# A state-space mixer in chunks of 256 tokens, recomputed in chunks of 128 with the state carried at each token tile

## The chip, the cores and the metric

The kernel runs on one core of one Trainium2 chip, as one launch. The metric is the device time of a whole execution in microseconds. A core has five engines that run their own instruction streams side by side: TensorE (PE: matmuls; its weight loads are listed as PEld), VectorE (DVE), ScalarE (ACT), GpSimd (POOL) and SyncE (SP, which only issues DMAs here). They wait for each other through semaphores. Matmuls write to PSUM, which has eight banks of 512 fp32 numbers in each of 128 partitions; everything else lives in SBUF.

## The reference, cut to what matters

The program is one transformer-like layer on 1024 tokens of width 1024: an input projection that feeds a sparse attention and a state-space mixer, a gated merge of both, and a feed-forward part. The change touches the state-space mixer alone. It has 32 heads of 64 channels in 8 groups of 4 heads; a group shares B and C with 128 states.

```
dt = softplus(dt_raw + dt_bias);  A = -exp(a_log);  X = xh * dt;  dA = dt * A
a_cum = cumsum(dA) within a chunk                       # chunk: any length gives the same result
CB = C B^T;  L[l, s] = exp(a_cum[l] - a_cum[s]) for s <= l, else 0
y_diag = (CB * L) X                                     # within the chunk
states = B^T (exp(a_cum[last] - a_cum) * X)             # what the chunk adds to the state
h(next chunk) = h * exp(a_cum[last]) + states           # the carried state
y_off = exp(a_cum) * (C h)                              # what the earlier chunks give
y = (y_diag + y_off + d_skip * xh) * silu(z)            # then a norm over all channels
```

The reference uses chunks of 64 tokens. The result doesn't depend on the length of a chunk, so a kernel may choose it: a longer chunk means larger triangles in y_diag, a shorter one more state updates.

## The kernel before

**Layout.** All activations are stored transposed, channels in the partitions and tokens in the free dimension, in halves of 512 tokens. The state-space part works in chunks of QC = 256 tokens, that is, two token tiles of 128 (P), so NCH = 4 chunks.

**Prologue (dt_part, L490).** It forms dt, dA, the running sum acum within each chunk of 256 (a triangular matmul, L507, plus a matmul with ones that adds the first tile's total to the second tile, L508), the chunk totals (L510 and L511), decay = exp(total - acum) and cdec = exp(total), one per chunk. It stores acum and exp(acum), transposed, to DRAM (d_ac and d_ea).

**The stage (L1086 to L1094).** The steps run over the 8 groups g, and in each group over the 4 chunks c: 32 steps. `weave` (L824) interleaves three generators by turns: `ssd_in` of this step, `ssd_out` of the step before, and `beside`, the filler, which is dense matmul work: the gate projection (L1059 to L1066, tile pw) and then the attention's output projection (L1074 to L1083, tile poa), 6 matmuls of 512 columns at a time (`dense_steps`, L231). Both have 128 turns of filler in all, four for a step.

**ssd_in (L949)** has four turns.
- It loads B^T, C^T and xs (tile ld), and the row acum broadcast over the partitions (al, L961). ACT computes exp(-relu(acum_s - acum_l)) from it in three pieces: for the source tokens of the first tile all 256 target tokens (in place in al, L967 and L969), for those of the second tile the 128 later ones (tile M, L966 and L969).
- PE multiplies B and C into the bank pcb: 256 columns for the first source tile (L972) and 128 for the second (L973). DVE applies a mask of 384 columns (triangle, ones, triangle; L975) to give cbm, and multiplies al and M by cbm (L977).
- PE transposes xs into px (L983); DVE multiplies by dt to give X (L985).
- Except in the last chunk, PE transposes B into pbn (L992), ACT copies it to bn (L994), and POOL forms Xd = X * decay (L996).

**ssd_out (L1000)** has four turns too.
- It loads z and, except in the first chunk, exp(acum), broadcast (d_ea, L1010), into yt (a part of tile zy). PE forms y_diag in the bank pyd: for each of two pairs of heads j, and each head e of a pair, which fills one half of the output rows, the first source tile gives 256 columns (L1016) and the second adds to the last 128 (L1017).
- Except in the last chunk, PE sums both tiles' state products in the bank pst (L1023, twice 256 columns).
- Except in the first chunk, PE forms C h in the bank pyo from the chunk's starting state st (L1028, twice 256 columns), and DVE computes yt = yt * pyo + pyd (L1030, L1031); the first chunk only copies pyd (L1033). DVE adds d_skip * xs (L1035), POOL multiplies by z (L1037), and the result is stored to d_y.
- ACT squares it and DVE sums the squares (L1041 to L1047). The state is updated: POOL multiplies st by cdec (L1051), DVE adds pst (L1053); the first chunk only copies pst (L1049).

**What sets the order.** The program's text gives the order in which instructions are offered; a planner (L55) then simulates all engines on a time line with its own cost estimates and chooses each engine's order from it. Only the parts under `in_order` keep the order of the text, and the state-space stage isn't one of them. On the chip each engine runs its list in that fixed order. PSUM banks are tiles of two pools: five banks (bank) for the state-space work, three (bank_d) for the dense matmuls. SBUF tiles come from arenas of equal slots (Q, R, EV, H), and a tile's first use waits until the slot's former tile has been read for the last time.

Of the kernel before, what the change touches and what calls it, by code (L numbers as in the profile page):

```python
# [10 lines left out]
F32 = mybir.dt.float32  # L11
# [6 lines left out]
P = 128  # L18
# [50 lines left out]
def build(tc, a, dbg=None, stop=99, slots=None):  # L69
# [117 lines left out]
    mask384 = con.tile([P, 384], F32, name="mask384")  # L187
    tri = mask384[:, 0:128]
# [186 lines left out]
    def const_loads():  # L375
        SP.dma_start(mask384, a["mask384"])
# [113 lines left out]
    def dt_part():  # L490
# [7 lines left out]
        for m in (15, 13, 11, 9, 7, 5, 3):  # L498
# [6 lines left out]
        pcv = pc[:, 0:256].rearrange("p (c t h) -> p c t h", c=NCH, t=2)  # L505
        dAv = dA.rearrange("p (c t) h -> p c t h", t=2)
        T.matmul(pc[:, 0:256], tri, dA.rearrange("p t h -> p (t h)"), start=True, stop=False)  # L507
        T.matmul(pcv[:, :, 1, :], ones, dAv[:, :, 0, :], start=False, stop=True)  # L508
        ptot = bank("ptot")
        T.matmul(ptot[:, 0:128], ones, dAv[:, :, 0, :], start=True, stop=False)  # L510
        T.matmul(ptot[:, 0:128], ones, dAv[:, :, 1, :], start=False, stop=True)  # L511
        acum = con.tile([P, NT, 32], F32, name="acum")
        V.tensor_copy(acum.rearrange("p t h -> p (t h)"), pc[:, 0:256])
        tot = tmp[1][:, 1, 0:NCH, :]
        V.tensor_copy(tot.rearrange("p c h -> p (c h)"), ptot[:, 0:128])
        decay = con.tile([P, NT, 32], F32, name="decay")
        V.tensor_tensor(decay.rearrange("p (c t) h -> p c t h", t=2), tot[:, :, None, :].to_broadcast([P, NCH, 2, 32]),
                        acum.rearrange("p (c t) h -> p c t h", t=2), op=OP.subtract)
        S.activation(decay, decay, AF.Exp)
        cdec = con.tile([P, NCH, 32], F32, name="cdec")  # L520
# [428 lines left out]
    def ssd_in(c, g, out):  # L949
# [12 lines left out]
        late_ = Q("M")  # L962
        Mv = [al[:, 0:2], al[:, 2:4], late_.rearrange("p (h l) -> p h l", h=4)]
        for h in range(4):
            hd = 4 * g + h
            S.activation(Mv[2][:, h], al[:, h, 128:256], AF.Relu, scale=-1.0, bias=acum[:, 2 * c + 1, hd:hd + 1])  # L966
            S.activation(al[:, h], al[:, h], AF.Relu, scale=-1.0, bias=acum[:, 2 * c, hd:hd + 1])  # L967
        for m in (al, Mv[2]):
            S.activation(m, m, AF.Exp, scale=-1.0)  # L969
        yield  # L970
        pcb = bank("pcb")
        T.matmul(pcb[:, 0:256], BT[:, 0:128], CT, start=True, stop=True)  # L972
        T.matmul(pcb[:, 256:384], BT[:, 128:256], CT[:, 128:256], start=True, stop=True)  # L973
        cbm = Q("cbm", (P, 384))
        V.tensor_tensor(cbm, pcb[:, 0:384], mask384, op=OP.mult)  # L975
        for m, cb in ((al, cbm[:, 0:256]), (Mv[2], cbm[:, 256:384])):
            V.tensor_tensor(m, m, cb[:, None, :].to_broadcast(list(m.shape)), op=OP.mult)  # L977
# [513 lines left out]
```

## Time and profile before

| | |
|---|---|
| median of 3 runs | 2521.27 us (2516.20 to 2521.45) |
| profiled execution, its own time | 2517.42 us |
| its span, from the first to the last instruction | 2515.6 us |
| granted clock of TensorE, mean over the span | 0.978 |
| matmul records on PE, all of the program | 11946 |
| DVE, ACT, POOL instructions | 3056, 2300, 833 |
| HBM read and written | 252.68 MB and 86.27 MB, 135 GB/s over the span |

The profile is one execution of the program. Its page gives the busy time of each engine as a share of the span; the chain of work that ended last, followed back from the last instruction to what released each step; and groups of instructions by line of the kernel, written as out<-in by the program's tile names, with partitions x elements, the count, the busy time, the mean length in ns, and the idle time of the engine just before them. A matmul's record lasts until its result has left the array, so records of back-to-back matmuls overlap, and PE can be busy all the time without being at its peak. The trace answers closer questions: windows (busy time of each engine in a stretch), waits (who waited for whom), and a timeline.

### The profile page before, as it was taken

How to read it: one execution, taken by the hardware profiler on the slowest of the kernel's cores; microseconds unless marked ns; L12 is line 12 of the kernel's file. 1: busy time of each engine (PE TensorE's matmuls, PEld its weight loads, DVE VectorE, ACT ScalarE, POOL GpSimd, SP SyncE). 2: the span in 40 equal slices, each digit the busy share in tenths (PEclk: the TensorE clock that was granted, in tenths of full speed). 3: DMA queues.
4: the chain of work that ended last, by engine and by line, in shares of the span. 5: the costliest groups of instructions: out<-in, count | busy, mean ns of one | idle time of the engine just before them, and what ended most of it. 6: DMA issues, size and time to landing. Idle time of an engine off the chain costs nothing.

```text
span 2515.6 us, 34898 instructions
## 1 busy us (share of the span) xinstructions
PE 2399.8 (95%) x11946; PEld 1941.1 (77%) x11946; DVE 1517.2 (60%) x3056; ACT 1214.0 (48%) x2300; POOL 1012.1 (40%) x833
## 2 busy tenths in 40 slices
PE   3999999989989999999999999999899999999997
PEld 2788888877768878777777777878777888888886
DVE  3356777499975664666457677355276666442326
ACT  3345666466545664555656656354344222343111
POOL 1332112433443332222245445666576555432233
PEclk7999999999999999999999999999999999999998
DMA  6124212533322222111568886554364444243132
GB/s 241 42 84 131 72 66 78 176 126 122 126 90 93 93 93 83 46 42 57 179 215 286 277 261 199 175 194 148 134 217 159 163 148 142 89 164 129 50 97 88
DMA packets 213026, 338.11 MB, mean 134 GB/s; under 512 B 22976, under 2 KB 87152, under 8 KB 212848
## 3 DMA queue, kind: packets, MB, share of 16 engines
q1 hardware_dynamic: 212128, 335.30, 40.0%
q8 instruction: 94, 1.54, 0.3%
q14 instruction: 84, 0.69, 0.1%
q10 hardware_dynamic: 720, 0.58, 0.1%
HBM read 252.68 MB, written 86.27 MB: 135 GB/s over the span
## 4 chain that ended last, share of the span: by engine, by line
PE 76%; DVE 12%; ACT 4%; DMA 3%; issue 3%; POOL 2%; SPq 0%; POOLq 0%; DVEq 0%; ACTq 0%
PE pw L227 15%; PE p L1254 14%; PE pfo L227 8%; PE pos L227 5%; PE plg L767 4%; PE poa L237 3%; PE pot L227 3%; PE pw L237 3%; PE po L816 3%; PE pt L800 3%; PE prel L584 2%; DVE junk L637 2%; PE puq L227 2%; PE pyd L1016 1%; DVE adas L319 1%
## 5 line engine op out<-in xcount | busy, mean ns | idle before, releaser
L153 POOL TENSOR_TENSOR wlo<-wraw,whi 128x512 fp32r<-128x512 f32 (+1 forms) x282 | 379.7, 1349 | 712.6 <-ACT whi L152 639.8
L152 ACT ACTIVATE whi<-wraw 128x512 fp32r<-128x512 f32 (+1 forms) x282 | 175.6, 624 | 375.8 <-PE pfo L227 114.7
L1254 PE MATMUL p<-xh,wr 128*128 128x512 f32 x880 | 275.6, 391 | 5.7 <-DVE g L1304 4.1
L1248 POOL TENSOR_TENSOR wr<-a,wr 128x512 fp32r<-128x512 f32 x110 | 154.4, 1416 | 118.3 <-ACT wr L1247 79.0
L1254 PEld LDWEIGHTS p<-xh,wr 128*128 128x128 f32 x880 | 165.8, 188 | 41.3 <-DVE g L1304 4.5
L1254 PE MATMUL p<-xl,wr 128*128 128x512 f32 x440 | 171.6, 390 | 0.0
L1247 ACT ACTIVATE wr<-a 128x512 fp32r<-128x512 f32 x110 | 67.9, 628 | 131.6 <-PE p L1254 110.1
L779 ACT ACTIVATE lg<-lg,mx 128x256 f32<-128x256 f32 (+7 forms) x128 | 98.3, 769 | 62.5 <-DVE mx L776 61.9
L227 PE MATMUL pfo<-ah,wlo 128*128 128x512 f32 x304 | 118.1, 389 | 0.0
L227 PE MATMUL pfo<-al,whi 128*128 128x512 f32 x304 | 117.9, 389 | 0.0
L227 PE MATMUL pfo<-ah,whi 128*128 128x512 f32 x304 | 117.8, 389 | 0.0
L639 ACT ACTIVATE junk<-acc,cand__2203 128x1024 bf16<-128x1024 f32 (+2 forms) x96 | 86.2, 897 | 58.3 <-DVE cand__2203 L682 25.1
L1254 PE MATMUL p<-h2h,wr 128*128 128x512 f32 x352 | 112.5, 396 | 0.0
L1369 DVE TENSOR_TENSOR facc<-facc,pfo 128x512 f32<-128x512 f32 x64 | 44.0, 687 | 112.0 <-PE pfo L227 112.0
L227 PE MATMUL pos<-yh,wlo 128*128 128x512 f32 x256 | 100.6, 394 | 1.9 <-POOL wlo L153 1.8
L318 POOL TENSOR_TENSOR adaw<-adaw,cs 128x512 f32<-128x512 f32 x64 | 70.2, 1103 | 77.8 <-DMA adaw<-ada_w 74.2
L590 DVE SCALAR_TENSOR_TENSOR acc<-rel,widx,acc 128x384 f32<-128x384 f32 (+2 forms) x90 | 87.1, 988 | 23.5 <-ACT rel L585 23.4
L227 PE MATMUL pos<-yh,whi 128*128 128x512 f32 x256 | 100.4, 393 | 0.6 <-ACT yh L1120 0.6
L585 ACT ACTIVATE rel<-prel 128x512 f32<-128x512 f32 (+3 forms) x160 | 77.2, 524 | 48.5 <-PE prel L584 45.0
L227 PE MATMUL pos<-yw,whi 128*128 128x512 f32 x256 | 99.8, 391 | 0.0
L800 PE MATMUL pt<-ident,lg 128*128 128x128 f32 x576 | 89.1, 278 | 7.7 <-ACT lg L779 7.0
L1254 PEld LDWEIGHTS p<-xl,wr 128*128 128x128 f32 x440 | 83.0, 189 | 17.2
(568 smaller groups left out, 7046.7 us busy)
## 6 DMA issues: line engine op xcount, KB each, us to landing
wraw<-w_in SPq DMA_DIRECT2D x130, 256.0 KB, 2.7
a<-w_ffn_in SPq DMA_DIRECT2D x120, 256.0 KB, 3.0
adaw<-ada_w SPq DMA_DIRECT2D x64, 256.0 KB, 3.2
al<-d_ac SPq DMA_DIRECT2D x32, 512.0 KB, 5.2
wraw<-w_o_ssd SPq DMA_DIRECT2D x64, 256.0 KB, 3.0
al<-d_a SPq DMA_DIRECT2D x44, 256.0 KB, 5.0
d_a<-g SPq DMA_DIRECT2D x38, 256.0 KB, 2.0
ada<-ada_p SPq DMA_DIRECT2D x16, 512.0 KB, 7.4
```

What stands on the lines that cost most here:

```text
L152: behind(S.activation(hi[:, :kt], raw[:, :kt], AF.Copy))
L153: behind(G.tensor_tensor(lo[:, :kt], raw[:, :kt], f(hi[:, :kt]), op=OP.subtract))
L227: T.matmul(o, wt[:, k0 + i, :], xs[k][xi][b][:, sl], start=pi == 0 and i == 0 and wt is hi and xi == 0, stop=pi == len(pcs) - 1 and i == l ...
L237: T.matmul(o, wt[:, k0 + j, :], xs[k][xi][b], start=i == 0, stop=i == 23)
L585: S.activation(rel[:, 512 * b:512 * b + w_], pr[:, 0:w_], AF.Relu)
L590: V.scalar_tensor_tensor(acc[i][:, 0:n], rel[:, 0:n], ws, acc[i][:, 0:n], op0=OP.mult, op1=OP.add)
L639: S.activation(jk, y, AF.Sign, scale=-1.0, bias=a_, accum_out=o)
L767: T.matmul(p[:, 0:w2], st[qi], KVT[ki][:, o_:o_ + w2], start=x == 0, stop=x == 2)
L779: S.activation(lg[:, 0:n], lg[:, 0:n], AF.Exp, scale=-1.0, bias=m, accum_out=mx[:, 3:4])
L800: T.transpose(ptv[:, hh, t, :], PR[hh, t][:, j * P:(j + 1) * P], ident)
L1248: G.tensor_tensor(w[:, 1], src, f(w[:, 0]), op=OP.subtract)
L1254: T.matmul(p, w[:, wi, i], X[x][i][xi], start=start and i == 0 and k == 0, stop=i == 3 and k == 2, skip_group_check=True)
```

## The change

The same stage works in chunks of 128 tokens, two to a step: the steps, their loads and their tiles stay those of 256 tokens.
- acum, the totals, decay and cdec are formed per tile of 128 tokens. The mask is one triangle of 128 x 128 (tri) instead of mask384.
- In ssd_in the exponentials cover only pairs within a tile: eight Relu pieces of 128 columns and one Exp; pcb has two matmuls of 128 columns; cbm has 256 columns, and one product with al replaces two. bn and Xd are formed in the last chunk too, for its first tile.
- In ssd_out, pyd has eight matmuls of 128 columns, none of which adds to another. pst holds the state products of the two tiles side by side. The new function `carried` forms mid, the state after the first tile: POOL multiplies st by the first tile's cdec, DVE adds the first half of pst (in the first chunk ACT copies it instead). pyo takes st for the first tile and mid for the second, 128 columns each; in the first chunk only the second tile. At the end of the step `carried` forms st from mid in the same way.
- exp(acum) is loaded in the first chunk too.

```diff
...
         V.scalar_tensor_tensor(dt, xd, 0.0, pl, op0=OP.max, op1=OP.add)
         V.scalar_tensor_tensor(dA, dt, -1.0, nA[:, None, :].to_broadcast([P, NT, 32]), op0=OP.mult, op1=OP.mult)
         pc = bank("pcum")
-        pcv = pc[:, 0:256].rearrange("p (c t h) -> p c t h", c=NCH, t=2)
-        dAv = dA.rearrange("p (c t) h -> p c t h", t=2)
-        T.matmul(pc[:, 0:256], tri, dA.rearrange("p t h -> p (t h)"), start=True, stop=False)
-        T.matmul(pcv[:, :, 1, :], ones, dAv[:, :, 0, :], start=False, stop=True)
+        dAf = dA.rearrange("p t h -> p (t h)")
+        T.matmul(pc[:, 0:256], tri, dAf, start=True, stop=True)
         ptot = bank("ptot")
-        T.matmul(ptot[:, 0:128], ones, dAv[:, :, 0, :], start=True, stop=False)
-        T.matmul(ptot[:, 0:128], ones, dAv[:, :, 1, :], start=False, stop=True)
+        T.matmul(ptot[:, 0:256], ones, dAf, start=True, stop=True)
         acum = con.tile([P, NT, 32], F32, name="acum")
         V.tensor_copy(acum.rearrange("p t h -> p (t h)"), pc[:, 0:256])
-        tot = tmp[1][:, 1, 0:NCH, :]
-        V.tensor_copy(tot.rearrange("p c h -> p (c h)"), ptot[:, 0:128])
+        tot = tmp[1][:, 1]
+        V.tensor_copy(tot.rearrange("p t h -> p (t h)"), ptot[:, 0:256])
         decay = con.tile([P, NT, 32], F32, name="decay")
-        V.tensor_tensor(decay.rearrange("p (c t) h -> p c t h", t=2), tot[:, :, None, :].to_broadcast([P, NCH, 2, 32]),
-                        acum.rearrange("p (c t) h -> p c t h", t=2), op=OP.subtract)
+        V.tensor_tensor(decay, tot, acum, op=OP.subtract)
         S.activation(decay, decay, AF.Exp)
-        cdec = con.tile([P, NCH, 32], F32, name="cdec")
+        cdec = con.tile([P, NT, 32], F32, name="cdec")
         S.activation(cdec, tot, AF.Exp)
         acT = [R("acT") for b in BS]
         for b in BS:
...
 
         al = R("al", (P, 4, QC))
         SP.dma_start(al, d_ac[c, hs][None].to_broadcast([P, 4, QC]))
-        late_ = Q("M")
-        Mv = [al[:, 0:2], al[:, 2:4], late_.rearrange("p (h l) -> p h l", h=4)]
         for h in range(4):
-            hd = 4 * g + h
-            S.activation(Mv[2][:, h], al[:, h, 128:256], AF.Relu, scale=-1.0, bias=acum[:, 2 * c + 1, hd:hd + 1])
-            S.activation(al[:, h], al[:, h], AF.Relu, scale=-1.0, bias=acum[:, 2 * c, hd:hd + 1])
-        for m in (al, Mv[2]):
-            S.activation(m, m, AF.Exp, scale=-1.0)
+            for t in range(2):
+                S.activation(al[:, h, P * t:P * t + P], al[:, h, P * t:P * t + P], AF.Relu, scale=-1.0,
+                             bias=acum[:, 2 * c + t, 4 * g + h:4 * g + h + 1])
+        S.activation(al, al, AF.Exp, scale=-1.0)
         yield
         pcb = bank("pcb")
-        T.matmul(pcb[:, 0:256], BT[:, 0:128], CT, start=True, stop=True)
-        T.matmul(pcb[:, 256:384], BT[:, 128:256], CT[:, 128:256], start=True, stop=True)
-        cbm = Q("cbm", (P, 384))
-        V.tensor_tensor(cbm, pcb[:, 0:384], mask384, op=OP.mult)
-        for m, cb in ((al, cbm[:, 0:256]), (Mv[2], cbm[:, 256:384])):
-            V.tensor_tensor(m, m, cb[:, None, :].to_broadcast(list(m.shape)), op=OP.mult)
-        out["M"] = Mv
+        for t in range(2):
+            T.matmul(pcb[:, P * t:P * t + P], BT[:, P * t:P * t + P], CT[:, P * t:P * t + P], start=True, stop=True,
+                     skip_group_check=True)
+        cbm = Q("cbm", (P, 2, P))
+        V.tensor_tensor(cbm, pcb[:, 0:256].rearrange("p (t l) -> p t l", t=2), tri[:, None, :].to_broadcast([P, 2, P]),
+                        op=OP.mult)
+        V.tensor_tensor(al, al, cbm.rearrange("p t l -> p (t l)")[:, None, :].to_broadcast([P, 4, QC]), op=OP.mult)
+        out["M"] = al
         yield
         px = bank("px")
         for t in range(2):
...
                         dt[:, 2 * c:2 * c + 2, hs, None].to_broadcast([P, 2, 4, 64]), op=OP.mult)
         out["X"] = X
         yield
-        if c < NCH - 1:
-            pbn = bank("pbn")
-            for t in range(2):
-                T.transpose(pbn[:, P * t:P * t + P], BT[:, P * t:P * t + P], ident)
-            bn = Q("bn", (P, 2, P))
-            S.activation(bn.rearrange("p t n -> p (t n)"), pbn[:, 0:256], AF.Copy)
-            Xd = Q("Xd", (P, 2, 4, 64))
-            G.tensor_tensor(Xd, X, decay[:, 2 * c:2 * c + 2, hs, None].to_broadcast([P, 2, 4, 64]), op=OP.mult)
-            out["bn"], out["Xd"] = bn, Xd
+        nt = 2 if c < NCH - 1 else 1
+        pbn = bank("pbn")
+        for t in range(nt):
+            T.transpose(pbn[:, P * t:P * t + P], BT[:, P * t:P * t + P], ident)
+        bn = Q("bn", (P, 2, P))
+        S.activation(bn[:, 0:nt], pbn[:, 0:P * nt].rearrange("p (t n) -> p t n", t=nt), AF.Copy)
+        Xd = Q("Xd", (P, 2, 4, 64))
+        G.tensor_tensor(Xd[:, 0:nt], X[:, 0:nt], decay[:, 2 * c:2 * c + nt, hs, None].to_broadcast([P, nt, 4, 64]), op=OP.mult)
+        out["bn"], out["Xd"] = bn, Xd
         yield
 
     def ssd_out(c, g, z):
...
         zy = R("zy", (P, 4, 256))
         zc, yt = zy[:, 0:2], zy[:, 2:4]
         SP.dma_start(zc, d_z[2 * g:2 * g + 2].rearrange("j p l -> p j l")[:, :, cl])
-        if c:
-            for e in range(2):
-                SP.dma_start(yt[64 * e:64 * e + 64],
-                             d_ea[c, hs].rearrange("(j e) l -> e j l", e=2)[e:e + 1].to_broadcast([64, 2, QC]))
+        for e in range(2):
+            SP.dma_start(yt[64 * e:64 * e + 64],
+                         d_ea[c, hs].rearrange("(j e) l -> e j l", e=2)[e:e + 1].to_broadcast([64, 2, QC]))
         pyd = bank("pyd")
         for j in range(2):
-            for e in range(2):
-                o = pyd[64 * e:64 * e + 64, 256 * j:256 * j + 256]
-                T.matmul(o, X[:, 0, 2 * j + e], M[j][:, e], start=True, stop=False, skip_group_check=True)
-                T.matmul(o[:, 128:256], X[:, 1, 2 * j + e], M[2][:, 2 * j + e], start=False, stop=True, skip_group_check=True)
+            for t in range(2):
+                for e in range(2):
+                    T.matmul(pyd[64 * e:64 * e + 64, 256 * j + P * t:256 * j + P * t + P], X[:, t, 2 * j + e],
+                             M[:, 2 * j + e, P * t:P * t + P], start=True, stop=True, skip_group_check=True)
             if j == 0:
                 yield
-        if c < NCH - 1:
-            pst = bank("pst")
-            for t in range(2):
-                T.matmul(pst[:, 0:256], z["bn"][:, t], z["Xd"][:, t].rearrange("p h n -> p (h n)"), start=t == 0, stop=t == 1)
+
+        pst = bank("pst")
+        for t in range(2 if c < NCH - 1 else 1):
+            T.matmul(pst[:, 256 * t:256 * t + 256], z["bn"][:, t], z["Xd"][:, t].rearrange("p h n -> p (h n)"),
+                     start=True, stop=True, skip_group_check=True)
+
+        def carried(to, st, t):
+            h4 = "p (h n) -> p h n"
+            G.tensor_tensor(to.rearrange(h4, h=4), st.rearrange(h4, h=4),
+                            cdec[:, 2 * c + t, hs, None].to_broadcast([P, 4, 64]), op=OP.mult)
+            V.tensor_tensor(to, to, pst[:, 256 * t:256 * t + 256], op=OP.add)
+
+        mid = Q("mid", (P, 256))
+        if c:
+            carried(mid, st, 0)
+        else:
+            S.activation(mid, pst[:, 0:256], AF.Copy)
         yield
-        if c:
-            pyo = bank("pyo")
+        pyo = bank("pyo")
+        for t, s_ in ((0, st), (1, mid)) if c else ((1, mid),):
             for j in range(2):
-                T.matmul(pyo[:, 256 * j:256 * j + 256], st[:, 128 * j:128 * j + 128], CT, start=True, stop=True)
-            ytf = yt.rearrange("p j l -> p (j l)")
-            V.tensor_tensor(ytf, ytf, pyo, op=OP.mult)
-            V.tensor_tensor(ytf, ytf, pyd, op=OP.add)
-        else:
-            S.activation(yt.rearrange("p j l -> p (j l)"), pyd, AF.Copy)
+                T.matmul(pyo[:, 256 * j + P * t:256 * j + P * t + P], s_[:, P * j:P * j + P], CT[:, P * t:P * t + P],
+                         start=True, stop=True, skip_group_check=True)
+        pv, po = (p.rearrange("p (j l) -> p j l", j=2) for p in (pyd, pyo))
+        on = slice(0 if c else P, QC)
+        V.tensor_tensor(yt[:, :, on], yt[:, :, on], po[:, :, on], op=OP.mult)
+        V.tensor_tensor(yt[:, :, on], yt[:, :, on], pv[:, :, on], op=OP.add)
+        if not c:
+            S.activation(yt[:, :, 0:P], pv[:, :, 0:P], AF.Copy)
         for j in range(2):
             V.scalar_tensor_tensor(yt[:, j, :], xs[:, j], dsk[:, 2 * g + j:2 * g + j + 1], yt[:, j, :],
                                    op0=OP.mult, op1=OP.add)
...
                 S.activation(ya_, sq[:, j], AF.Copy)
             else:
                 V.tensor_tensor(ya_, ya_, sq[:, j], op=OP.add)
-        if c == 0:
-            S.activation(st, pst[:, 0:256], AF.Copy)
-        elif c < NCH - 1:
-            G.tensor_tensor(st.rearrange("p (h n) -> p h n", h=4), st.rearrange("p (h n) -> p h n", h=4),
-                            cdec[:, c, hs, None].to_broadcast([P, 4, 64]), op=OP.mult)
-            V.tensor_tensor(st, st, pst[:, 0:256], op=OP.add)
+        if c < NCH - 1:
+            carried(st, mid, 1)
         yield
 
     def beside():
```

More of the change, by code (lines that the diff above doesn't have):

```diff
@@ L186, in build @@
     ident = con.tile([P, P], F32, name="ident")
-    mask384 = con.tile([P, 384], F32, name="mask384")
-    tri = mask384[:, 0:128]
+    tri = con.tile([P, P], F32, name="tri")
     dtb = con.tile([P, 32], F32, name="dtb")
@@ L375, in const_loads @@
     def const_loads():
-        SP.dma_start(mask384, a["mask384"])
+        SP.dma_start(tri, a["tri"])
         SP.dma_start(dtb, a["dt_bias"][None, :].to_broadcast([P, 32]))
@@ L1468, in arrays_of @@
     out["ident"] = np.eye(P, dtype=f32)
-    tri = np.triu(np.ones((P, P), f32))
-    out["mask384"] = np.concatenate([tri, np.ones((P, P), f32), tri], 1)
+    out["tri"] = np.triu(np.ones((P, P), f32))
     oh = np.zeros((32, 384), f32)
```

## The prediction

> **What bounds the kernel now.** I read the page first, for the engine that is full and for the chain that ended last; then the table of windows over the stage that the change rewrites, TensorE's (PE's) waits in that stage, PE's timeline through one step, and the groups of instructions by line.
>
> ```profile
> span 2515.6 us, 34898 instructions
> ...
> PE 2399.8 (95%) x11946; PEld 1941.1 (77%) x11946; DVE 1517.2 (60%) x3056; ACT 1214.0 (48%) x2300; POOL 1012.1 (40%) x833
> ...
> PE 76%; DVE 12%; ACT 4%; DMA 3%; issue 3%; POOL 2%; SPq 0%; POOLq 0%; DVEq 0%; ACTq 0%
> ```
>
> PE is busy 95% of the span and makes up 76% of the chain. That is an average, so the windows of the state-space stage decide (about 1195 to 1562 us). The columns are length, busy time of PE, of its weight loads (PEld), of DVE, ACT and POOL, the granted clock, the DMA share and GB/s.
>
> ```profile
> 1215.00:1340.00 125.00, 125.00 (x684) 97.59 (x683) 71.81 (x114) 74.62 (x166) 47.61 (x39) 1.00 0.66 213
> 1340.00:1365.00 25.00, 21.30 (x111) 14.79 (x110) 16.06 (x22) 17.08 (x37) 12.45 (x10) 0.92 0.85 273
> 1365.00:1540.00 175.00, 175.00 (x944) 136.52 (x944) 134.38 (x190) 110.76 (x241) 82.37 (x62) 0.99 0.82 269
> 1540.00:1562.00 22.00, 20.12 (x113) 15.71 (x112) 16.70 (x27) 11.53 (x22) 10.02 (x9) 1.00 0.50 156
> 1195.00:1562.00 367.00, 360.94 (x1961) 278.46 (x1962) 244.89 (x361) 226.49 (x491) 155.17 (x122) 0.99 0.73 236
> ```
>
> PE has no idle time in 300 of the 367 us. It loses 3.7 us in the second row and 1.9 us in the fourth. DVE (245 of 367 us), ACT (226) and POOL (155) have room. PE's waits in this stage say the same (us in total, times, longest):
>
> ```profile
> PE poa L237 <- ACT ath L247: 2.0, 2, 1.8
> PE pyd L1016 <- DVE al L977: 1.5, 2, 1.3
> PE poa L237 <- POOL atl L248: 1.2, 1, 1.2
> ...
> PE pos L227 <- ACT yh L1120: 0.6, 1, 0.6
> ```
>
> Only the second belongs to the state-space work itself. So what PE has to stream sets the pace here, and the sum is made in PE time. One step (one group of heads, 256 tokens) on PE's timeline (start, us, instruction, number of records):
>
> ```profile
> 1409.46 0.66 PE L1016 MATMUL pyd<-al,X 128*64 128x256 f32 x4
> 1409.94 0.40 PE L1017 MATMUL pyd<-M,X 128*64 128x128 f32 x4
> 1410.27 0.70 PE L972 MATMUL pcb<-ld 128*128 128x256 f32 x2
> 1410.80 0.38 PE L973 MATMUL pcb<-ld 128*128 128x128 f32 x2
> 1411.12 0.66 PE L1016 MATMUL pyd<-al,X 128*64 128x256 f32 x4
> 1411.60 0.40 PE L1017 MATMUL pyd<-M,X 128*64 128x128 f32 x4
> 1411.92 1.13 PE L1023 MATMUL pst<-Xd,bn 128*128 128x256 f32 x4
> 1412.89 0.60 PE L983 MATMUL px<-ident,ld 128*128 128x128 f32 x4
> 1413.33 1.03 PE L1028 MATMUL pyo<-ld,state 128*128 128x256 f32 x4
> 1414.01 0.58 PE L237 MATMUL poa<-atl,whi 128*128 128x512 f32 x1
> ```
>
> **Prices of a pass.** An fp32 matmul leaves two records here (two passes; two matmuls at L1028 make x4), a transpose leaves one. Records overlap, so a pass costs the distance to the next start, not its record's length. Two records of 128 columns take 0.38 us (L973) and four take 0.60 us (L983): 0.11 us for each further one, so **a 128-column pass costs 0.109 us** (I use 0.44 / 4, from L983's start to L1028's). Four passes of 256 columns take 1.03 us (L1028): 0.43 us more than four of 128, so **a 256-column pass costs 0.108 us more, 0.217 us**. The pyd matmuls fill half of the output rows each, and the two halves run side by side: four records of L1017 span 0.40 us, no more than two of L973. So time goes by columns.
>
> **The change on PE.** There are 32 steps: four chunks c in each of eight groups.
> - Scores within the chunk (pcb): 256 + 128 columns become 128 + 128; two passes shrink by 0.108 us: 0.22 us a step.
> - Output within the chunk (pyd): for each of the two j, a side-by-side pair of 256 and one of 128 become two of 128; two passes shrink: 0.43 us a step.
> - Together 0.65 us x 32 = **20.8 us removed**.
> - Carried output (pyo): where c > 0, two matmuls of 256 become four of 128, 8 x 0.109 us for 4 x 0.217 us: nothing. Where c = 0, two of 128 are new: 4 x 0.109 x 8 = 3.5 us.
> - State products (pst): the same columns where c < 3. Where c = 3 one of 256 is new: 2 x 0.217 x 8 = 3.5 us, with one transpose, 0.109 x 8 = 0.9 us. **7.9 us added.**
> - The prologue's running sums (L507 to L511): 640 columns become 512, 0.2 us removed, once.
>
> Net on PE: 20.8 + 0.2 - 7.9 = **13.1 us less**.
>
> **The change on the other engines**, by these groups (busy, mean ns | idle before):
>
> ```profile
> L967 ACT ACTIVATE al<-al,acum 128x256 f32<-128x256 f32 x128 | 54.8, 494 | 0.0
> ...
> L966 ACT ACTIVATE M<-al,acum 128x128 f32<-128x128 f32 x128 | 40.4, 387 | 0.0
> ...
> L977 DVE TENSOR_TENSOR M<-M,cbm 128x512 f32<-128x512 f32 x32 | 24.6, 769 | 8.3 <-ACT M L969 8.0
> ...
> L1028 PEld LDWEIGHTS pyo<-ld,state 128*128 128x128 f32 x96 | 16.4, 190 | 1.5 <-issue 0.2
> ...
> L1051 POOL TENSOR_TENSOR state<-state,cdec 128x256 f32<-128x256 f32 x16 | 11.5, 718 | 47.6 <-PE pyo L1028 32.4 <-DMA d_y<-zy 7.3 <-DMA zy<-d_z 4.6
> ...
> L1053 DVE TENSOR_TENSOR state<-state,pst 128x256 f32<-128x256 f32 x16 | 6.6, 414 | 0.0
> ```
>
> ACT: 128 Relus fall from 494 to 387 ns (14 us less), and a 512-column Exp a step goes too. DVE: the second product goes (769 ns x 32 = 25 us), 32 more state additions come (414 ns, 13 us), and at c = 0 two half-tile operations (16 x 0.41 us, 7 us, by the same row). POOL: 32 more products of 718 ns (23 us) and eight half-size Xd, which I bound between 0.4 us (the DVE row) and 1.4 us (twice the POOL row): 155 becomes about 185 of 367 us. The cover for all of it is PE's stream, so I cost it at nothing. Without that cover POOL's 30 us would count, but POOL would have to double first to become the bound.
>
> **The new wait.** Within a step, the second half of pyo now needs the state carried to the middle of the chunk: a POOL product of the old state (ready early), then a DVE addition that waits for pst. If PE reaches those matmuls first, everything queued behind them on PE stands, px, pbn and the dense matmuls; on DVE, X and the products for the next step stand behind the addition, and on POOL wlo and Xd behind the product. Before, state and use were a whole step apart. DVE's rows show what the addition may queue behind:
>
> ```profile
> 1415.34 1.22 DVE L977 TENSOR_TENSOR al<-al,cbm 128x1024 f32<-128x1024 f32 x1
> 1416.47 0.41 DVE L1053 TENSOR_TENSOR state<-state,pst 128x256 f32<-128x256 f32 x1
> ```
>
> At best 0.41 us passes after pst, and PE has px (0.44 us) and the first half of pyo (0.44 us) to run meanwhile: no loss. At worst the addition sits behind a whole al product, 1.22 + 0.41 - 0.88 = 0.75 us of PE a step, 24 us in all. The order is planned with such waits in view, and the nearest row, PE waiting for a DVE product of the step (pyd behind al), lost 1.5 us over all 32 steps. I take 1.5 us.
>
> **The ends of the stage.** In the last row of the windows PE waits for the last steps' chain, which gets longer; the saving of the last four steps (0 to 2.6 us) may stay there. I take half, 1.3 us back. In the second row PE waits for ACT and POOL; one gets lighter, the other heavier, so the 3.7 us could vanish or stay; I take no change. The start loads a mask smaller by 128 KB; I take nothing.
>
> **Sum:** -13.1 + 1.5 + 1.3 = **-10.3 us**. Against the profiled execution (2517.42 us, 1.8 us of it outside the span) that is 2507.1. That execution lies 3.9 us under the median of the three runs, 2521.27; from the median it is 2511.0. I forecast from the mean of the four, 2519.1: **2509**.
>
> **The rivals.**
> 1. *PE waits for the mid-chunk state.* Price up to 24 us; from 0.41 us a step (13.1 / 32) it eats the whole gain. At 0.75 us: -13.1 + 24 + 1.3 = +12, 2531. For: the new chain runs through three in-order engines. Against: the existing waits on DVE hardly ever reach PE, and dense matmuls lie ready to be put between.
> 2. *Transfers pace the second half.* The third window has a DMA share of 0.82 at 269 GB/s, and d_ea now comes at c = 0 too:
>
> ```profile
> zy<-d_ea SPq DMA_DIRECT2D x48, 128.0 KB, 4.0
> ```
>
> That is 16 more of these, 2 MB. If DMA allowed no faster pace, the 16 or so steps of that window would lose their 0.41 us each, 6.6 us: -3.7, 2515. Against: no wait of PE in the list has a DMA for its releaser.
> 3. *The lighter ACT also ends the loss at 1340 to 1365 us:* -10.3 - 3.7 = -14, 2505. For: the longest PE wait is for ACT. Against: PE also waited for POOL there, which gets more to do.
> 4. *Short passes don't hide their weight loads.* If a pass with 128-wide weights can't be shorter than the 190 ns that its load's record lasts, 0.081 us is added to eight passes of pyo where c > 0 (24 steps, 15.6 us), four where c = 0 (2.6 us) and two of pcb (32 steps, 5.2 us): -10.3 + 23.4 = +13, 2532. Against: L973's passes follow each other after 0.11 us, with a load for each.
>
> On this fourth rival the Trainium skill, "TensorE: Matmul & The Clock Gate", Part 3, "The mechanism", says that a weight load overlaps matmuls in flight only where the row groups differ. By that rule, and the 107 ns that the same page's section on LDWEIGHTS gives for 128 columns, the change's 152 additional loads would cost an estimated 16 us, and the sum would be +6 us instead of -10.3. The trace disagrees: the four px passes are 0.11 us apart, all of it their own columns.
>
> **How the numbers follow.** The forecast has 0.56, and I give the rivals 0.14, 0.13, 0.11 and 0.06. A measurement tells about 0.2% (5 us) from no change. The forecast's own range, with the bounds of its small terms, is 2503 to 2515, nearly all of it faster; rival 3 is faster; rival 2 mostly the same, with a third faster; rival 1 goes from the same to slower; rival 4 is slower. That makes 0.66 faster, 0.16 the same, 0.18 slower. The range runs from rival 3 with the runs' spread (2499) to half of rival 1's price (2525).
>
> **What would show it.** Right: in the window from the first pcb to the last step, L1016 and L1017's successors at 0.65 us less a step, PE still without idle time, the stage about 10 us shorter, the rest of the program at its old length. Wrong: a wait of PE (pyo) for the DVE addition in most steps (rival 1); PE waits released by DMA after 1365 us (2); records of pyo 0.19 us apart (4). It would be wrong in another way if the planned order moved elsewhere and the time changed outside this stage.

## The result, and the profile after

| | before | after |
|---|---|---|
| median | 2521.36 us (4 runs, 2516.20 to 2523.48) | 2554.85 us (4 runs, 2552.93 to 2557.56) |
| after / before | | 1.0139 (95%: 1.0126 to 1.0153) |
| span of the profiled execution | 2515.6 us | 2551.6 us |

The change makes the kernel slower by about 34 us; the prediction was 2509 us, between 2499 and 2525. The page of the changed kernel, its span and its engines:

```profile
span 2551.6 us, 35252 instructions
...
PE 2399.3 (94%) x12094; PEld 1951.1 (76%) x12094; DVE 1517.3 (59%) x3072; ACT 1183.8 (46%) x2276; POOL 1039.9 (41%) x873
```

The span grew by 36.0 us while PE is as busy as before (2399.3 and 2399.8 us). So the loss is idle time of PE, and the windows say where. (The chain of waits of this profile breaks off near the program's end, so it is not used.) Columns as in the prediction: length, busy time of PE, PEld, DVE, ACT, POOL, granted clock, DMA share, GB/s. Windows of the changed kernel over the state-space stage and what follows it:

```profile
1190.00:1338.00 148.00, 146.82 (x876) 117.23 (x877) 77.87 (x123) 74.78 (x183) 62.45 (x58) 1.00 0.64 201
1338.00:1507.00 169.00, 151.22 (x855) 120.63 (x854) 108.14 (x163) 81.85 (x191) 79.18 (x66) 0.95 0.81 257
1507.00:1600.00 93.00, 72.43 (x416) 57.82 (x415) 64.58 (x95) 42.48 (x97) 53.63 (x44) 0.90 0.59 184
1600.00:1796.00 196.00, 192.01 (x845) 157.04 (x844) 90.63 (x104) 85.34 (x145) 121.26 (x89) 0.99 0.49 170
```

The same windows of the kernel before:

```profile
1190.00:1338.00 148.00, 146.83 (x820) 112.47 (x819) 79.69 (x139) 91.64 (x203) 50.33 (x42) 1.00 0.63 203
1338.00:1507.00 169.00, 165.29 (x882) 127.24 (x881) 124.60 (x181) 104.82 (x226) 77.47 (x59) 0.98 0.86 278
1507.00:1600.00 93.00, 91.02 (x465) 72.48 (x464) 59.45 (x79) 49.81 (x98) 53.85 (x42) 1.00 0.56 188
```

The first row is as good as before. In the second PE idles 17.8 us instead of 3.7, in the third 20.6 instead of 2.0, at a granted clock of 0.95 and 0.90 instead of 0.98 and 1.00. PE's waits in this part (us in total, times, longest), changed kernel:

```profile
PE pyo L1033 <- ACT mid L1028: 10.1, 2, 6.7
PE pos L226 <- ACT whi L152: 7.9, 2, 4.0
PE pst L1015 <- ACT bn L987: 7.3, 4, 3.1
PE prn L271 <- POOL r L265: 4.6, 1, 4.6
PE pyd L1008 <- DVE al L970: 3.8, 3, 1.9
...
PE pyo L1033 <- DVE mid L1022: 0.9, 1, 0.9
```

The wait of rival 1, pyo for the DVE addition, comes to 0.9 us, once. The waits for ACT are longer, but few. The two in the second window, for the copies mid and bn, come to 17.4 us, nearly all of PE's idle time there; the third, for whi, is 7.9 us. That's not the whole loss. For the rest of it, compare first and last starts of the dense output projection (poa) with those of the steps' score matmuls (pcb). Kernel before (line, operation, names, count: length in ns least/median/most, first and last start in us):

```profile
L237 PE MATMUL poa<-ath,wlo x128: 387/389/628, 1358.9 to 1514.5; 128*128 128x512 f32 x128
...
L973 PE MATMUL pcb<-ld x64: 272/275/421, 1198.7 to 1544.7; 128*128 128x128 f32 x64
...
L227 PE MATMUL pos<-yh,wlo x256: 387/389/582, 1515.2 to 1760.4; 128*128 128x512 f32 x128
```

Changed kernel:

```profile
L236 PE MATMUL poa<-ath,wlo x128: 387/392/632, 1346.1 to 1506.7; 128*128 128x512 f32 x128
...
L965 PE MATMUL pcb<-ld x128: 270/275/426, 1191.3 to 1575.2; 128*128 128x128 f32 x128
...
L226 PE MATMUL pos<-yh,wlo x256: 387/389/796, 1507.4 to 1796.0; 128*128 128x512 f32 x128
```

The changed kernel is through with its dense filler 7.8 us earlier (1506.7 against 1514.5), but with its steps 30.5 us later (1575.2 against 1544.7). For 68.5 us, instead of 30.2, steps run with no filler of their own left. The filler is a fixed stock: 128 turns of 6, 768 matmuls, 24 for each of the 32 steps. Counted in the trace, the dense matmuls that had started before the first pyd of step 8, 16 and 24 were 258, 460 and 674 before, and 280, 491 and 747 after; by this count the stock was gone by step 28 before and by step 25 after (steps counted from 0). What is dense and comes next, pos, can start on the groups whose y is ready, but not end before the last step has given its y.

**The loss in one sum.** I charged every matmul that starts between the last one of the attention (plg) and the last of pos with its columns: 0.227 us for a pass of 512 columns of the dense matmuls (their starts in the timeline are 0.23 us apart), 0.216 for 256, 0.109 for 128, half of that for the side-by-side ones of pyd. Idle time is from the trace; the rest of the stretch (a lower clock, breaks between kinds of matmul) is what is left.

| us | stretch | PE's columns | idle | rest |
|---|---|---|---|---|
| before | 570.0 | 526.5 | 8.7 | 34.8 |
| after | 611.0 | 513.9 | 44.3 | 52.8 |

So PE's work did fall, by 12.6 us, idle time rose by 35.6 and the rest by 18.0: +41.0. The last plg starts 5.6 us earlier than before (1184.9 against 1190.5), and what follows pos is as long as before (755.2 us before, 755.6 after), which gives the 36 us of the span.

The idle time can be split at poa's last start, where the filler ends. Before, 4.9 us lie ahead of it and 3.8 behind it; in the changed kernel 19.8 ahead and 24.6 behind. So 20.8 of the 35.6 us belong to the bare end, and 14.9 to a time when filler was still in stock: there PE stood, for 17.4 us in all, at instructions that waited for ACT's copies.

### The profile page after: what moved, and what is told of

The parts are those of the page before. It is cut to its first block, busy times and chain, and to the rows that moved or that the text cites. A ratio compares the mean times of both kernels' runs of the same rounds, so it can differ in the third digit from the quotient of the medians.

```text
span 2551.6 us, 35252 instructions
## 1 busy us (share of the span) xinstructions
PE 2399.3 (94%) x12094; PEld 1951.1 (76%) x12094; DVE 1517.3 (59%) x3072; ACT 1183.8 (46%) x2276; POOL 1039.9 (41%) x873
## 5 line engine op out<-in xcount | busy, mean ns | idle before, releaser
L774 ACT ACTIVATE lg<-lg,mx 128x256 f32<-128x256 f32 (+7 forms) x128 | 98.2, 769 | 57.3 <-DVE mx L771 56.7
L959 ACT ACTIVATE al<-al,acum 128x128 f32<-128x128 f32 x256 | 78.9, 389 | 88.8 <-DMA al<-d_ac 88.8
L580 ACT ACTIVATE rel<-prel 128x512 f32<-128x512 f32 (+3 forms) x160 | 77.2, 524 | 47.8 <-PE prel L579 44.3
```

What stands on the lines that cost most here:

```text
L580: S.activation(rel[:, 512 * b:512 * b + w_], pr[:, 0:w_], AF.Relu)
L774: S.activation(lg[:, 0:n], lg[:, 0:n], AF.Exp, scale=-1.0, bias=m, accum_out=mx[:, 3:4])
L959: S.activation(al[:, h, P * t:P * t + P], al[:, h, P * t:P * t + P], AF.Relu, scale=-1.0, bias=acum[:, 2 * c + t, 4 * g + h:4 * g + h + 1])
```

## The experiments

Five theories were set against each other, the last two only after e1 to e4; the expectations name them by their letters or their words. **A**: al's tile is given free too late, its load (d_ac) lands late, and ACT stands. **B**: the new link itself, the state at the middle of the chunk. **C**: the 16 additional d_ea loads. **D**: the planned order spends the filler too early. **E**: six PSUM banks in every step, where a group's first and last chunk had needed five and four, so that steps overlap less. A came from ACT's waits, changed kernel:

```profile
ACT al L959 <- DMA al<-d_ac: 88.8, 29, 7.6
```

and from ACT's timeline at the longest stall of PE, where mid is copied behind eight Relus that waited 5.08 us for that load (start, us, operation, [idle before, releaser]):

```profile
1349.89 2.44 ACT L959 ACTIVATE al<-al,acum 128x128 f32<-128x128 f32 x8 [5.08 <-DMA al<-d_ac]
1352.24 0.61 ACT L1048 ACTIVATE ysqt<-zy 128x512 f32<-128x512 f32 x1
1352.76 0.36 ACT L1028 ACTIVATE mid<-pst 128x256 f32<-128x256 f32 x1
```

Ratios are to the kernel before, in runs on the same chip (its median was 2520.3 us beside e1 to e4, 2519.6 beside e5 to e8, 2520.2 beside e9 to e12). Idle and rest are worked out as in the sum above, from the profiled execution of each run (that of e6, 2526.81 us, is one of its slower ones); the last two columns are the last starts of poa and pcb.

| run | median us | ratio (95%) | idle | rest | poa | pcb |
|---|---|---|---|---|---|---|
| e1_al_in_q | 2607.35 | 1.0344 (1.0328 to 1.0359) | 77.6 | 67.7 | 1514.7 | 1632.8 |
| e2_al_three | 2555.26 | 1.0141 (1.0124 to 1.0158) | 45.0 | 50.6 | 1517.5 | 1584.3 |
| e3_before_two | 2524.15 | 1.0018 (1.0005 to 1.0031) | 13.6 | 35.5 | 1514.1 | 1545.5 |
| e4_no_mid | 2511.19 | 0.9963 (0.9948 to 0.9978) | 15.0 | 37.3 | 1512.6 | 1519.0 |
| e5_five_banks | 2603.23 | 1.0332 (1.0315 to 1.0348) | 71.4 | 74.9 | 1494.4 | 1622.8 |
| e6_text_order | 2522.04 | 1.0013 (1.0000 to 1.0025) | 22.0 | 44.7 | 1545.6 | 1534.6 |
| e7_before_text_order | 2538.68 | 1.0073 (1.0056 to 1.0090) | 26.3 | 40.1 | 1547.2 | 1540.0 |
| e8_five_banks_text_order | 2524.50 | 1.0016 (1.0007 to 1.0026) | 23.3 | 41.9 | 1541.4 | 1530.4 |
| e9_text_mid_dve | 2513.39 | 0.9977 (0.9967 to 0.9987) | 17.5 | 38.4 | 1528.2 | 1516.5 |
| e10_state_first | 2541.51 | 1.0084 (1.0068 to 1.0101) | 33.9 | 52.2 | 1493.4 | 1566.5 |
| e11_state_first_text | 2534.27 | 1.0060 (1.0045 to 1.0075) | 32.1 | 44.9 | 1548.3 | 1541.4 |
| e12_text_six | 2563.78 | 1.0180 (1.0159 to 1.0201) | 48.4 | 59.8 | 1482.1 | 1593.6 |

**e1_al_in_q.** al in two tiles of the other arena (Q), with a load of two heads each; the Exp and the product go by tile.

```diff
-        al = R("al", (P, 4, QC))
-        SP.dma_start(al, d_ac[c, hs][None].to_broadcast([P, 4, QC]))
+        als = [Q("al", (P, 2, QC)) for _ in range(2)]
+        for i, al in enumerate(als):
+            SP.dma_start(al, d_ac[c, 4 * g + 2 * i:4 * g + 2 * i + 2][None].to_broadcast([P, 2, QC]))
```

> The changed kernel with the broadcast row al in two 512-column tiles of the roomy arena Q instead of one tile of R, so that its load no longer waits for a slot of R. Theory A (late rows: al's tile comes free late, its load starts 5 us instead of 13 us ahead of use, ACT stands 89 us for it, and the copies behind it that PE needs come late): ACT's wait for al falls under 15 us, PE's idle time in the state-space stage from 39 us to under 12 us, time 2500 to 2515 us. Theory B (the new chain through the mid-chunk state holds PE): PE's idle time stays over 30 us, time 2545 to 2558 us. Theory C (the 2 MB of additional d_ea loads): 2545 to 2558 us as well, with PE waits on DMA.

It was slower than the changed kernel by 52 us, which no theory had expected. Its bare end is longer still, 118 us from poa to pcb, and the stock of dense matmuls was gone by step 21. But PE also waits in many steps for the product with al, a wait of 3.8 us in the changed kernel:

```profile
PE pyd L1011 <- DVE al L973: 37.0, 20, 7.4
```

ACT's wait for al didn't fall below 15 us, it rose to 123.3. So this run tests neither A nor the order.

**e2_al_three.** Three tiles for al, set apart for it alone and taken in turn.

```diff
+    al_tiles = [R(f"al{i}", (P, 4, QC)) for i in range(3)]
...
-        al = R("al", (P, 4, QC))
+        al = al_tiles[(NCH * g + c) % 3]
```

> The changed kernel with three fixed tiles of R for al, taken in turn; the other two kinds of R tiles (ld, zy) share the remaining five. Theory A: al's load starts three steps after the last use rather than two, ACT's wait for al falls under 20 us, time 2500 to 2520 us, unless ld or zy become late in their five tiles, which would show as ACT or POOL waits on those loads. Theories B and C: 2545 to 2558 us.

No change from the changed kernel, 2555.26 and 2554.85. But ACT's wait for the load rose too, so what A would gain from an early al wasn't tested:

```profile
ACT al L960 <- DMA al<-d_ac: 106.1, 28, 8.7
```

**e3_before_two.** The opposite: the kernel before, with its al held to two tiles in turn.

```diff
-        al = R("al", (P, 4, QC))
+        al = al_tiles[(NCH * g + c) % 2]
```

> The kernel before, otherwise unchanged, with only two fixed tiles of R for al. Theory A: the chunk of 256 gets the same illness: ACT's wait for al rises from near 0 to over 50 us, and the time by 10 to 40 us, 2530 to 2560 us. Theories B and C, which blame the chunk of 128: no change, 2518 to 2525 us.

Only 0.2% slower (1.0005 to 1.0031). But ACT's wait for al came to 7.2 us, not to over 50:

```profile
ACT M L967 <- DMA al<-d_ac: 7.2, 4, 2.7
```

So two tiles don't make al late in the kernel before, and this run leaves A open too. What speaks against A as the whole cause are e4 and e6 below: there ACT waits for al 48.5 and 61.6 us, and the time is far lower.

**e4_no_mid.** From the second chunk of a group on, both halves of pyo take the chunk's starting state; all other instructions stay.

```diff
-        for t, s_ in ((0, st), (1, mid)) if c else ((1, mid),):
+        for t, s_ in ((0, st), (1, st)) if c else ((1, mid),):
```

> The changed kernel with both halves of the carried output taken from the state at the step's start, where c > 0; that leaves the mid-chunk state out of the output there, while its products and additions stay. Theory A: al stays late, so ACT still waits over 60 us for it and the time stays at 2535 to 2558 us. Theory B: PE no longer waits within a step, time 2500 to 2515 us. Theory C: 2545 to 2558 us.

It ran 44 us faster than the changed kernel, and 0.4% faster than before. Every matmul, load and DVE, ACT and POOL operation is still there, so C falls, and so does any theory of more work on an engine. A single dependency, in 24 of the 32 steps, makes the difference: B, and the time that it forecast, but not as rival 1 had it, since PE hardly waits at that dependency. With the dependency goes the bare end, because the planner chose another order: idle time behind the filler's end is 5.6 us instead of 24.6, and ahead of it 9.3 instead of 19.8. Windows of e4:

```profile
1507.00:1600.00 93.00, 90.44 (x447) 73.83 (x446) 47.97 (x67) 39.76 (x72) 59.34 (x47) 1.00 0.51 167
```

and its last starts, poa and pcb:

```profile
L236 PE MATMUL poa<-ath,wlo x128: 387/389/628, 1359.9 to 1512.6; 128*128 128x512 f32 x128
...
L965 PE MATMUL pcb<-ld x128: 275/275/377, 1192.3 to 1519.0; 128*128 128x128 f32 x128
```

Steps and filler end within 6.4 us of each other. At steps 8, 16 and 24, 230, 397 and 624 dense matmuls had started (280, 491 and 747 in the changed kernel). ACT still waits 48.5 us for al here; a wait of that size doesn't by itself cost the time.

**e5_five_banks.** The transposes of B go into the unused half of pcb's bank, right behind the score matmuls, and the copy to bn with them.

```diff
+            T.transpose(pcb[:, 256 + P * t:256 + P * t + P], BT[:, P * t:P * t + P], ident)
...
+        S.activation(bn[:, 0:nt], pcb[:, 256:256 + P * nt].rearrange("p (t n) -> p t n", t=nt), AF.Copy)
...
-        pbn = bank("pbn")
```

> The changed kernel with the two transposes of B moved up to the scores, into the free half of their PSUM bank, and the copy bn with them: five banks a step instead of six, for the five there are. Theory D (the order planned for PE: the chain of a step got longer, the plan fills the time with dense matmuls, 33 a step for 24 that there are, so they run out at step 25 and the last steps stand bare): by itself this changes nothing unless the chain gets shorter, 2540 to 2558 us. Theory E (PSUM banks: pyd and pst are held through the mid-chunk chain, so the next step's tiles come late): dense matmuls last until step 28 or later, time 2500 to 2518 us.

48 us slower than the changed kernel, outside both ranges. The bare end is the longest of all, 128 us: the planner found another order, and a worse one. That doesn't settle E; e8 below does, with the same edit without the planner's hand in PE's order.

**e6_text_order and e7_before_text_order.** PE's order in this stage is held to that of the text, four filler turns a step; e6 is the changed kernel, e7 the kernel before.

```diff
-    if True:
+    with in_order(mybir.EngineType.PE):
         prev = None
```

> The changed kernel with PE's order in the state-space stage fixed to that of the program's text, which puts 24 dense matmuls into each of the 32 steps; the other engines stay planned. Theory D: all steps are covered alike, none stands bare at the end, and if the chain of a step can run in the 10.4 us that PE needs for it, PE is idle under 12 us in the stage, time 2503 to 2520 us. If the step's own chain can't go below some 12 us (theory B in its strong form), PE waits in every step, and the time stays at 2535 to 2558 us. Theory E: PE waits in every step for banks, 2535 to 2558 us.

> The kernel before with PE's order in the state-space stage fixed to that of the text. Theory D: its planned order already covers 28 of 32 steps, so little changes, 2514 to 2528 us; if this order is better or worse by itself, the difference shows here and has to be taken off from the run of the changed kernel in that order.

Both came out slower than theory D had it (e6 by 2 us, e7 by 11), and PE's idle time in e6 is 22.0 us, not under 12. But the pair separates the change from the order. In one and the same order the change gains: 2522.04 against 2538.68, 16.6 us. The planner's order was worth 19 us to the kernel before (2519.6 beside this run against 2538.7) and cost the changed kernel 33 us (2554.9 against 2522.0). Of e6's idle time 19.3 us lie ahead of the filler's end, as in the changed kernel (19.8), and 2.7 behind it instead of 24.6: what the text's order takes away is the bare end. e6 starts 222, 414 and 606 dense matmuls by steps 8, 16 and 24, and poa now ends after pcb:

```profile
L236 PE MATMUL poa<-ath,wlo x128: 388/396/632, 1371.1 to 1545.6; 128*128 128x512 f32 x128
...
L965 PE MATMUL pcb<-ld x128: 271/275/583, 1203.4 to 1534.6; 128*128 128x128 f32 x128
```

**e8_five_banks_text_order.** The edits of e5 and e6 together.

> The changed kernel with both: five banks a step and PE's order of the text. Theory D: as the text order alone, 2503 to 2520 us. Theory E: faster than the text order alone by over 10 us.

2524.50, nearly as e6 and 4.5 us above D's range. One bank fewer is worth nothing in a fixed order, and the 79 us between e5 and e8 are the order alone.

**e9_text_mid_dve.** e6's longest wait of PE for a step is the first chunk's copy of mid on ACT:

```profile
PE pyo L1033 <- ACT mid L1028: 12.0, 5, 3.5
```

The copy goes to DVE, on top of e6:

```diff
-            S.activation(mid, pst[:, 0:256], AF.Copy)
+            V.tensor_copy(mid, pst[:, 0:256])
```

> The changed kernel in PE's text order (2522 us) with the copy of the mid-chunk state in the first chunk moved from ACT to DVE. Theory D: the 12.0 us that PE waited there for ACT's copy, which stands behind the Relus that wait for al, mostly vanish: 2508 to 2516 us. Rival: the copy is late because pst is late, and DVE's copy is as late: 2518 to 2526 us.

8.6 us faster than e6, and 0.2% faster than the kernel before (0.9967 to 0.9987): apart from e4 the fastest kernel here. The wait for ACT's copy is gone, and that for DVE's is small (e9):

```profile
PE poa L236 <- ACT ath L246: 6.2, 1, 6.2
PE pyo L1033 <- DVE mid L1022: 2.4, 2, 2.1
```

Here is what is left of A: ACT waits for al 57.3 us in e9 too, and it costs only what stands behind it on ACT's queue and PE needs soon.

**e10_state_first and e11_state_first_text.** The block that forms pst and mid moves ahead of pyd in ssd_out, so that the chain to mid starts earlier: in the planned order (e10), and with e9's two edits (e11).

```diff
+        pst = bank("pst")
...
+            S.activation(mid, pst[:, 0:256], AF.Copy)
         pyd = bank("pyd")
...
-        pst = bank("pst")
...
-            S.activation(mid, pst[:, 0:256], AF.Copy)
```

> The changed kernel, planned order, with the state products pst and the mid-chunk state offered at the head of ssd_out, ahead of pyd rather than behind it. Theory D with B (the step's chain through the mid-chunk state is what stretches the planned step): two turns lie between the state and its use, the planned step shortens, dense matmuls last until step 28 or later, 2500 to 2525 us. If the plan stretches the steps for another reason, 2540 to 2560 us.

> The state products first, the first chunk's copy on DVE, and PE's order of the text. Theory D: no wait of PE for the mid-chunk state is left, 2500 to 2514 us. Rival: PE waits for Xd or bn instead, which are now needed a turn earlier, 2518 us or more.

e10 gains 13 us on the changed kernel, but lies in the second of its ranges: the stock was gone by step 24, not 28, and the bare end is 73 us, longer than the changed kernel's 68.5. So an earlier start of the chain doesn't make the planner spread the filler. What fell is the idle time ahead of the filler's end, from 19.8 to 11.7 us (behind it, 22.2 instead of 24.6): the waits for the copies mid and bn went from 17.4 us to 1.6. They are the second part of the loss. e11 went as its rival said and loses 21 us against e9, since pst now comes before its inputs are ready. PE's waits of e11:

```profile
PE pst L1006 <- ACT bn L987: 12.3, 8, 2.5
...
PE pst L1006 <- POOL Xd L989: 6.9, 7, 2.1
```

**e12_text_six.** e6 with six filler turns a step rather than four: the same instructions in an order of the text that only spends the filler faster, which is D by itself.

```diff
-            weave(ssd_in(*s_, z) if s_ else iter(()), 4 if s_ else 0, ssd_out(*prev) if prev else iter(()), 4 if prev else 0, filler, 4)
+            weave(ssd_in(*s_, z) if s_ else iter(()), 4 if s_ else 0, ssd_out(*prev) if prev else iter(()), 4 if prev else 0, filler, 6)
```

> The changed kernel in PE's text order, but with six turns of dense matmuls to a step instead of four, so that they run out after two thirds of the steps. Theory D: the last ten or so steps stand bare as in the planned order, PE's idle time comes back at the end of the stage, 2540 to 2575 us. Rival (where the dense matmuls stand is of no weight, the planned order lost its time to waits in all steps): 2515 to 2530 us.

42 us slower than e6, 9 us slower than the changed kernel. Windows of e12, and its last starts:

```profile
1507.00:1620.00 113.00, 90.48 (x489) 69.83 (x490) 71.64 (x114) 51.65 (x121) 53.30 (x50) 0.83 0.62 191
```

```profile
L236 PE MATMUL poa<-ath,wlo x128: 386/394/629, 1338.8 to 1482.1; 128*128 128x512 f32 x128
...
L965 PE MATMUL pcb<-ld x128: 269/275/584, 1199.2 to 1593.6; 128*128 128x128 f32 x128
```

Filler that is gone 111 us before the last step brings back the signature of the changed kernel: PE idle for 22.5 us in this window and a granted clock of 0.83. So an early end of the filler costs this much by itself, in an order of PE that no planner chose: D is shown, as the larger part of the loss. e4 shows that the mid-chunk link is what makes the planned order end it early. The smaller part, ahead of the filler's end, is not D.

## Why the prediction was wrong, point by point

**The prices on PE and the net of 13.1 us: right.** By columns PE's work fell by 12.6 us; that sum is made with nearly the prediction's own prices, so it checks the count alone. The prices are borne out in one order, where the kernel gained 16.6 us (e6 against e7; by the two intervals 8 to 23), and by the rows below. Rival 4, a loss of 13 us, is out with it. PE's timeline of the changed kernel, within a step:

```profile
1286.88 0.71 PE L965 MATMUL pcb<-ld 128*128 128x128 f32 x4
1287.53 0.66 PE L1008 MATMUL pyd<-al,X 128*64 128x128 f32 x8
1288.11 0.70 PE L1015 MATMUL pst<-Xd,bn 128*128 128x256 f32 x2
```

One half of pyd takes 0.58 us from its start to the next; before, the two kinds of the same half took 0.81 (1409.46 to 1410.27). That is 0.23 us less, and the prediction had 0.43 for both halves. The 128-wide passes of pcb span 0.71 us for four records; at 0.19 us a load they would have spanned more than 0.27 + 3 x 0.19 = 0.84.

**The failed step is "The new wait".** It put the longer chain at 1.5 us because "the order is planned with such waits in view", and rival 1 was played down because "dense matmuls lie ready to be put between". Both look at one step's gap, and not at 32. Filler put into one step's wait is taken from a later one, since there are 24 dense matmuls a step (24 x 0.227 = 5.4 us) and no more. The longer chain of a step was indeed covered: by (747 - 491) / 8 = 32 dense matmuls a step between steps 16 and 24, where before there were (674 - 460) / 8 = 27. The bill came in the last seven steps, which ran bare: 24.6 us of idle time behind the filler's end instead of 3.8, and 33 us of the kernel's time, by e6. Rival 1 named the right link and a price (+12) of the right sign, but put it in the wrong place, at PE's wait for the addition in every step (0.9 us in all). Its 24 us counted the addition in 32 steps, though only 24 have one; in the other eight mid is a copy on ACT, which the step didn't price, and for two of those PE waited 10.1 us. The forecast's upper end, 2525, is half of this rival's net of 12 us, not of its price of 24, which would give 2519.

**The ends of the stage: far too small.** 1.3 us stood for the last steps' longer chain. The end was priced with the stage's present length of bare steps (30 us), and the change itself more than doubled that (68 us).

**The other engines at no cost: half right.** The counts hold: ACT fell by 30 us (1214.0 to 1183.8), POOL rose by 28 (1012.1 to 1039.9), and DVE is equal, where the prediction's terms give 5 us less (its products with al got longer, as the last section shows). But the cover named for it, PE's stream, is what ran out. One cost of ACT was overlooked: mid of the first chunk is copied there behind Relus that wait for a load, 10.1 us of PE in the changed kernel, and 8.6 us by e9 against e6.

**Rival 2, transfers, and rival 3: not seen.** e4 has the same loads and is fast. PE has no wait for a load in the list; only through ACT, whose copies stand behind the Relus that wait for al, does one reach it. The loss in the second window grew instead of ending.

**What stays open.** Why the planner's own time line needs more filler for a step with the mid link than the chip does (in the order of the text 24 a step are enough) was not tried: no run changed its estimates. That its estimate of the link is too long is an inference from e4 and e6, and e10 doesn't support it: an earlier start of the link left the stock as short. Why al's load lands late, and what ACT's copies cost in the planned order by themselves, wasn't measured either: e1 to e3 didn't bring al in earlier, and e9 moved the copy in the order of the text only (8.6 us).

## What to carry to other kernels

Work that fills gaps is a stock: count it per step, and ask of a longer chain in every step when the stock will be gone, not whether one step's gap is covered. Where a planner orders the work, a small new dependency can change the whole order, so time the edit in a fixed order too; the difference tells the edit's own worth (here -16.6 us) from that of the order (here 33 us against it). And look at who stands first in the queue of the engine that makes a short but urgent copy.

## What the runs showed of the hardware that was not expected

**The clock falls behind idle time.** PE stood 6.66 us before 1353.17. Windows of the changed kernel around it:

```profile
1346.00:1353.00 7.00, 0.51 (x2) 0.07 (x1) 1.90 (x4) 3.11 (x10) 0.00 (x0) 0.71 0.98 332
1353.00:1358.00 5.00, 4.83 (x28) 4.08 (x28) 4.92 (x7) 4.58 (x10) 4.71 (x4) 0.50 1.06 316
1358.00:1365.00 7.00, 7.00 (x36) 5.90 (x36) 6.96 (x8) 4.00 (x9) 6.28 (x5) 0.91 1.05 348
1365.00:1375.00 10.00, 9.98 (x59) 7.78 (x58) 8.19 (x12) 6.68 (x15) 8.47 (x8) 1.00 1.03 351
```

For the 5 us after the gap PE worked at half its clock, and about another 0.6 us went in the next row (0.09 x 7), so this wait cost some 3 us more than its length. The Trainium skill, "TensorE: Matmul & The Clock Gate", Part 1, "What's actually happening", says that an idle window of about 3.4 us halves the clock until as long a busy one has passed. These rows agree in kind, a gap of 6.66 us and then half the clock; at 0.50 over 5 us it lasted longer than one such window. The lower clock, 0.95 and 0.90 in the windows above, is part of why the rest rose by 18 us beside the idle time.

**DVE and POOL take turns at these products.** Groups of the changed kernel, over the stage (busy, mean ns | idle before):

```profile
L970 DVE TENSOR_TENSOR al<-al,cbm 128x1024 f32<-128x1024 f32 x32 | 55.9, 1747 | 1.5
...
L1020 POOL TENSOR_TENSOR mid<-state,cdec 128x256 f32<-128x256 f32 x24 | 31.6, 1316 | 0.0
```

The shortest of these DVE products took 1.21 us, and a POOL product beside an idle DVE took 0.60 (at 1543.21); where the two overlapped they took 1.99 and 1.60 (at 1570.48 and 1571.35). The times fit engines that take turns. Of the 32 products on DVE, 24 started while POOL was at work on an operation, and each ended 1.08 or 1.09 us after that operation; the one at 1570.48 did so behind POOL's wlo (1570.12, 1.27 us). The other eight took 1.21 or 1.22 us, and where POOL started behind one of them (Xd, 0.16 us after the product at 1549.25), POOL's operation took 1.95 us; the median of the 32 is 1.04. The prediction priced POOL's product at 0.72 us. PE's waits for either come to 4.7 us (3.8 + 0.9), so this is not the loss in itself, though it lengthens the new link on the chip: in the changed kernel half of the 24 mid products took 1.59 us or more, in e9 half of them 0.61 or less.
